# A retention head's epsilon moved to VectorE, and the gates' scalings of two heads moved behind later evictions

## The chip, the cores and the metric

The kernel runs on one core of one Trainium2 chip. Its engines work side by side, each through its own queue in order: TensorE (matrix products, PE in the profile, with its weight loads as PEld), VectorE (DVE), ScalarE (ACT), GpSimd (POOL) and SyncE (SP, which here only asks for transfers). The metric is the time of one execution on the device in microseconds. Lower is better.

## What is computed

Two layers of an encoder over 512 frames of width 1024, in float32. Each layer norms its input, multiplies it by one large matrix, and feeds two branches: four mLSTM heads, and four retention heads of value width 512. Both are merged through gates, and a feed-forward part and an embedding follow. The change concerns the retention branch, cut here to its core:

```python
def head_layernorm(y, g, n_heads):          # per frame and head, over 512 values
    mu = jnp.mean(yf, axis=-1, keepdims=True)
    var = jnp.mean(jnp.square(yf - mu), axis=-1, keepdims=True)
    yn = ((yf - mu) * lax.rsqrt(var + EPS)).reshape(B, S, W)
    return yn * g.astype(jnp.float32)
...
hr = retention_chunkwise(rq4, rk4, rv, log_gamma)
y_r = silu(rg) * head_layernorm(hr, r_norm_g[i], R_HEADS)
merged = sigmoid(gm) * (y_m @ w_bm[i]) + sigmoid(gr) * (y_r @ w_br[i])
```

## The kernel before

The 512 frames are held as 4 blocks of 128. Every product with a float32 operand is made as three matmuls of a high and a low part (`fp32r`). So each weight that is loaded (tiles `wr`) is split before use: ScalarE copies the high part (L309), VectorE subtracts it for the low part (L310), into tiles `w`, `w_A` to `w_D` or `w_t` with three slots of the large kind. TensorE needs both parts.

Most large products are formed by seven partial products, P1 to P7 (one level of Strassen's scheme). `run_pair` makes them for two column tiles at a time in the order P1, P5, P6, P2, P3, P7, with P4 put off to the next `flush()`. `run_wide` makes them for values and gates, 2 heads at a time, in two halves `u` each, P1 and P5 first, then P6 and P2 in turns, then P7, P3, P4. After a product `done` takes it out of PSUM: P1, P6 and P7 and P4 share a bank "a", so P6 can't start before P1 has been taken out, and P4 not before P7. In `pair_tiles` these evictions are lines 610 to 622, inside `ahead()`, which raises their priority.

The order in which an engine works is made at compile time from the order of the program text, priorities and dependencies. The text order is one input to it and not the order itself.

Retention heads are handled in turn. `r_attend` multiplies scores by values, one block `j` after the other: TensorE makes the block, ScalarE copies it to `num[:, j, :]` (L845), and `each(j)` follows:
- VectorE takes the statistics of the block (`bn_stats` L1154, `bn_aggr` L1155) into `mv`
- GpSimd adds EPS to the variance (L1157) and raises it to -1/2 (L1158) into `hv`, both 128x1
- where a gate is given, `r_gate` for an earlier block: ScalarE scales the gate by `hv` (L1200), VectorE forms (num - mean) x gate in place (L1201)

Gates come from `r_gates` for two heads at once. For the first and the third head of a layer (`r_attend(0, ...)` and `r_attend(2, ...)`, which end before) `r_gate` follows each finished gate within `r_gates`. The second and the fourth head (`r_attend(1, ...)` and `r_attend(3, ...)`, which come after) get the other gate `g` as an argument, and each runs `r_gate` for blocks 0 and 1 inside `each(2)` and `each(3)`. What remains comes behind: for the second head blocks 2 and 3 right after `r_attend`, ahead of the next value products `rv_vals(2)`; for the fourth head behind P6 and P2 of the first gr pair. `r_out` then transposes `num` on TensorE (L867): for the second head in the middle of `rv_vals(2)` (ahead of P7), for the fourth right after P7 of the gr pair, with P4 of that pair flushed after the first group of transposes.

GpSimd also asks for the transfers that add weight blocks in DRAM (L367, tiles `s...t`), each of which waits for a certain matmul. VectorE forms the last operands of `rv_vals` itself (L474).

The tiles `y` of `rv_vals` and `r_gates` take turns in four buffers of the tags `qkh` and `qkl`, in the order in which they are made. The gates `g` are such tiles.

Of the kernel before, what the change touches and what calls it, by code (L numbers as in the profile page):

```python
# [35 lines left out]
F32 = mybir.dt.float32  # L36
F32R = mybir.dt.float32r
AF = mybir.ActivationFunctionType
OP = mybir.AluOpType
# [3 lines left out]
P = 128  # L43
T = 512
NT = T // P
# [4 lines left out]
EPS = 1e-6  # L50
# [203 lines left out]
def build(ctx, tc, ins, out):  # L254
    nc = tc.nc
    ve, ac, gp, te = nc.vector, nc.scalar, nc.gpsimd, nc.tensor
# [17 lines left out]
    cur = {}  # L274
# [96 lines left out]
    def pace():  # L371
        if at["step"] < len(steps) and at["credit"] >= 0:
            step()
# [6 lines left out]
    def next_unit():  # L380
        n = at["unit"]
        at["unit"] += 1
        tick("FULL" if full(n) and units[n][0] == "PAIR" else units[n][0])
        return n
# [130 lines left out]
    def flush():  # L515

        while later:
            later.pop()()
# [35 lines left out]
            product(x)  # L554
        later.append(last)

    def run_wide(name, act, done, mid=None):

        n = next_unit()
        assert units[n][0] == "WIDE", units[n]  # L560
        bank = {}
        for x, u in TURNS:
            y, j = WIDE[x]
            if u and x != "P6":
                tick("WIDE")
            if (x, u) == ("P6", 0):
                flush()
            if (x, u) == ("P7", 0) and mid:
                mid()
            b = {"P2": "b", "P5": "c", "P3": "c"}.get(x, "a")  # L570
            first = x in ("P1", "P2", "P5")
            if first and u == 0:
                bank[b] = [ps(f"{name}{b}{t}") for t in range(2)]
            ready(place[n, (y, u)] + LOOK)
            wh, wl = pieces.pop((n, (y, u)))
            for k in (2 * u, 2 * u + 1):
                h, l = act[k](j)
                s = slice(k % 2 * T, (k % 2 + 1) * T)
                f, e = first and k == 0, k == 3
                for t in range(2):  # L580
                    ts = slice(t * P, (t + 1) * P)
                    o = bank[b][t]
                    te.matmul(o, h[:, ts], wh[:, s], start=f, stop=False, skip_group_check=True)
                    te.matmul(o, h[:, ts], wl[:, s], start=False, stop=False, skip_group_check=True)
                    cur["mm"] = te.matmul(o, l[:, ts], wh[:, s], start=False, stop=e, skip_group_check=True)  # L585
            if u:
                for t in range(2):
                    done(x, t, bank[b][t])
            pace()

    def ahead():
# [369 lines left out]
    x = big("x0", F32)  # L961
# [22 lines left out]
    for i in range(L):  # L984
# [38 lines left out]
        for k in range(KT):  # L1023
            s = slice(k * P, (k + 1) * P)
            f, e = k == 0, k == KT - 1
# [119 lines left out]
        def r_attend(h, pt, vv, g=None):  # L1145
            nm = f"l{i}r{h}"
            num = cur["low"].tile([P, NT, 512], F32, name=f"{nm}num", tag="num")
            st = cols.tile([P, NT, 6], F32, name=f"{nm}st", tag="st")
            mv = cols.tile([P, NT, 2], F32, name=f"{nm}mv", tag="mv")
            hv = cols.tile([P, NT], F32, name=f"{nm}hv", tag="hv")  # L1150
            norm = num, mv, hv

            def each(j):
                ve.bn_stats(st[:, j, :], num[:, j, :])  # L1154
                ve.bn_aggr(mv[:, j, :], st[:, j, :])  # L1155
                c = hv[:, j:j + 1]
                gp.tensor_scalar(c, mv[:, j, 1:2], EPS, None, OP.add)  # L1157
                gp.tensor_tensor(c, c, nhalf[:, 0:1], OP.pow)  # L1158
                if g and j > 1:
                    r_gate(norm, g, j - 2)  # L1160

            attend(nm, pt, vv[0], vv[1], 0, 512, num, each)
            return norm
# [33 lines left out]
        def r_gate(norm, g, j):  # L1197

            num, mv, hv = norm
            ac.activation(g[j], g[j], AF.Copy, scale=hv[:, j:j + 1])  # L1200
            ve.scalar_tensor_tensor(num[:, j, :], num[:, j, :], mv[:, j, 0:1], g[j], OP.subtract, OP.mult)  # L1201

        def r_out(h, num, y):
            nm = f"l{i}r{h}o"
            for v in range(4):
                o = back(nm, num, v)
                if v == 0:
                    flush()
                k = (4 * h) % 8 + v
                c = bcol(i, "grn", 4 * h + v)  # L1210
                ac.activation(y[0][k], o, AF.Copy, scale=c)
                ve.scalar_tensor_tensor(y[1][k], o, c, y[0][k].bitcast(F32), OP.mult, OP.subtract)
# [15 lines left out]
        low = cur["br"].tile([P, KT, T], F32R, name=f"l{i}xnl", tag="xn")  # L1228
# [21 lines left out]
            return [[cur["low"].tile([P, 576], F32R, name=f"{nm}v{a}{j}", tag=f"v{a}", bufs=NT) for j in range(NT)]  # L1250
                    for a in "hl"]

        def rv_vals(h, mid=None):

            nm = f"l{i}r{h}"
            bv = [tmp(f"{nm}bv{d}") for d in range(2)]
            for d in range(2):
                nc.sync.dma_start(bv[d], bias_rows(1024 + (h + d) * 512))
            y = [[cur["low"].tile([P, T], F32, name=f"{nm}y{d}{j}", tag="qk" + "hl"[d], bufs=4) for j in range(NT)]
                 for d in range(2)]  # L1260
            v = value_tiles(nm)

            def head0(j):
                split(y[0][j], v[0][j][:, :T], v[1][j][:, :T])

            def head1(j):
                gp.dma_start(rv_dram[i, h // 2, j], y[1][j])

            def done(x, t, o):
                a, b = t, 2 + t  # L1270
                if x == "P1":
                    ve.tensor_tensor(y[0][b], o, bv[0], OP.add)
                elif x == "P2":
                    ve.tensor_tensor(y[0][b], o, y[0][b], OP.add)
                    head0(b)
                elif x == "P4":
                    ve.tensor_tensor(y[0][a], o, bv[0], OP.add)
                    head0(a)
                elif x == "P5":
                    ve.tensor_tensor(y[1][a], o, bv[1], OP.subtract)  # L1280
                elif x == "P6":
                    ve.tensor_tensor(y[1][b], o, bv[1], OP.subtract)
                elif x == "P3":
                    ve.scalar_tensor_tensor(y[1][b], o, -1.0, y[1][b], OP.mult, OP.subtract)
                    head1(b)
                else:
                    ve.scalar_tensor_tensor(y[1][a], o, -1.0, y[1][a], OP.mult, OP.subtract)
                    head1(a)

            run_wide(f"{nm}v", xs, done, mid)  # L1290
            return v

        def rv_fetch(h):
# [11 lines left out]
        qk = qk_tiles(f"l{i}m0")  # L1305
# [15 lines left out]
        vv = mv_vals(0, xa, n1.c)  # L1321
# [4 lines left out]
        pt = m_scores(0, qk)  # L1326
        qk = m_qk(1, xa, n1, xn_tile)
        num = m_attend(0, pt, vv)
# [9 lines left out]
        xs = sevenfold(xn, xs_t)  # L1338
        pt = m_scores(1, qk)
        qk = m_qk(2, xn, None)  # L1340
        xs_sums(0)
        num = m_attend(1, pt, vv)
        gs = m_gates(1, xn, None)
        vv = mv_vals(1, xn, None, lambda: m_back(1, gs, num))
        xs_sums(1)
        pt = m_scores(2, qk)
        qk = m_qk(3, xn, None)
        xs_sums(2)
        num = m_attend(2, pt, vv)
# [4 lines left out]
        pt = m_scores(3, qk)  # L1354
        gs = m_gates(3, xn, None)
        num = m_attend(3, pt, vv)
        vv = rv_vals(0, lambda: m_back(3, gs, num))


# [15 lines left out]
        qk = r_qk(0)  # L1375
# [4 lines left out]
        pt = r_scores(0, qk)  # L1380
        qk = r_qk(1)
        num = r_attend(0, pt, vv)
        vv = rv_fetch(1)
        pt = r_scores(1, qk)
        g = r_gates(0, num, lambda: rv_split(vv))
        yr = acts(cur["br"], f"l{i}yr0")
        r_out(0, num[0], yr)
        num = r_attend(1, pt, vv, g)
        for j in (2, 3):
            r_gate(num, g, j)  # L1390
        vv = rv_vals(2, lambda: r_out(1, num[0], yr))
        qk = r_qk(2)

        def br_tiles(c0, c1):
# [7 lines left out]
        pt = r_scores(2, qk)  # L1402
        qk = r_qk(3)
        num = r_attend(2, pt, vv)
        vv = rv_fetch(3)
        br_tiles(4, 8)
        pt = r_scores(3, qk)
        g = r_gates(2, num, lambda: rv_split(vv))
        yr = acts(cur["br"], f"l{i}yr1")
        r_out(2, num[0], yr)  # L1410
        num = r_attend(3, pt, vv, g)
        mh, ml = [], []
        gr = {}

        def gr_gates(p, then=None):
            def consume(g):
                for d in range(2):
                    ac.activation(g[d], g[d], AF.Sigmoid, bias=bcol(i, "bgr", 2 * p + d), scale=SIGN[d])
                    gr[2 * p + d] = g[d]

            pair_tiles(f"l{i}gr{p}", xs, consume, then=then)

        gr_gates(0, {"P6": lambda: r_gate(num, g, 2), "P2": lambda: r_gate(num, g, 3)})
        r_out(3, num[0], yr)
        for c in range(KT):
            if c and c % 2 == 0:
# [3 lines left out]
            u = tmp(f"l{i}bml{c}")  # L1430
# [15 lines left out]
        if i == L - 1:  # L1446
            x_pool = phase("x", act_side)
            whole = x_pool.tile([P, KT, T], F32, name=f"l{i}x", tag="x")
            x = [whole[:, c, :] for c in range(KT)]
        else:  # L1450
            x = big(f"l{i}x", F32)
# [355 lines left out]
```

## Time and profile before

| | us |
|---|---|
| median of 3 runs | 2301.65 |
| lowest, highest | 2300.31, 2305.29 |
| the profiled execution | 2302.19 |
| its span in the profile | 2300.5 |

The profile is of one execution. It gives busy times by engine, a list of waits (who waited for whom, total, times, longest), and the instructions of each engine in order of time: start, duration, engine, line, operation, output and inputs, and in brackets the idle time before it with what ended it. Matmuls are pipelined: the duration of one overlaps the next, and the pace is read from their starts. The durations on GpSimd are rough. Tiles are named by layer and head, counted from 0: `l0r1num` is `num` of layer 0, second retention head; `l0gr0` the first gr pair; `l0r2v` the value products of `rv_vals(2)`.

### The profile page before, as it was taken

What the parts mean: (1) busy time and instruction counts of PE and PEld (TensorE: products, weight loads), DVE (VectorE), ACT (ScalarE), POOL (GpSimd) and SP (SyncE); (2) the same over time, 40 slices, a digit from 0 to 9 for tenths busy, and PEclk for the clock granted to TensorE, in tenths of its full rate; (3) what the DMA queues carried; (4) which work ended last, traced back from release to release, by engine and by line L of the source; (5) the groups of instructions that cost most, each with busy time, mean ns of one, the idle gap of its engine ahead of it and who ended that gap; (6) DMA issues with size and microseconds to landing.
All of it is one profiled execution on the core that took longest, in us unless ns stands there. A gap on an engine that the chain in (4) does not pass through costs nothing.

```text
span 2300.5 us, 36407 instructions
## 1 busy us (share of the span) xinstructions
PE 2277.2 (99%) x13532; PEld 2020.8 (88%) x13532; DVE 1759.0 (76%) x2690; ACT 1266.5 (55%) x1835; POOL 616.2 (27%) x984
## 2 busy tenths in 40 slices
PE   9999999999999999999999999999999999999998
PEld 7888899888888899999888888988888888999997
DVE  7877767886676878788779687777867678787785
ACT  6766544554554546556557564445545446566564
POOL 3332222223124322223432332221232242111112
PEclk9999999999999999999999999999999999999999
DMA  6776787787789888888886768876877898878741
GB/s 211 189 195 175 243 234 215 209 235 211 233 228 268 220 229 229 239 239 210 227 227 183 196 177 250 232 213 220 228 221 208 244 266 217 246 233 232 236 161 56
DMA packets 187890, 499.33 MB, mean 217 GB/s; under 512 B 26352, under 2 KB 29808, under 8 KB 187712
## 3 DMA queue, kind: packets, MB, share of 16 engines
q0 software_dynamic: 57520, 188.53, 36.9%
q1 hardware_dynamic: 114496, 280.97, 36.2%
q10 hardware_dynamic: 15696, 27.50, 3.6%
q8 instruction: 106, 1.74, 0.3%
q14 instruction: 72, 0.59, 0.1%
HBM read 478.03 MB, written 194.51 MB: 292 GB/s over the span
## 4 chain that ended last, share of the span: by engine, by line
PE 85%; DVE 7%; ACT 2%; issue 2%; DMA 2%; POOL 1%; SPq 0%; DVEq 0%; ACTq 0%; POOLq 0%
PE l0f L488 1%; PE l0f L489 1%; PE l0f L490 1%; PE l0br L488 1%; PE l1br L488 1%; PE l1br L490 1%; PE l0br L490 1%; PE l1br L489 1%; PE l0br L489 1%; DVE w_B L310 1%; PE l1f L488 1%; PE l1f L490 1%; PE l1f L489 1%; DVE w_C L310 1%; PE l0pg L488 1%
## 5 line engine op out<-in xcount | busy, mean ns | idle before, releaser
L309 ACT ACTIVATE w<-wr 128x1024 fp32r<-128x1024 f32 (+1 forms) x193 | 199.7, 1042 | 125.9 <-issue 28.5
L310 DVE TENSOR_TENSOR w<-wr,w 128x1024 fp32r<-128x1024 f32 (+1 forms) x193 | 233.8, 1214 | 45.3 <-ACT w L309 44.7
L309 ACT ACTIVATE w_B<-wr 128x1024 fp32r<-128x1024 f32 x123 | 130.4, 1060 | 150.5 <-PE l0bm L490 13.1
L310 DVE TENSOR_TENSOR w_B<-wr,w_B 128x1024 fp32r<-128x1024 f32 x123 | 150.0, 1221 | 55.0 <-ACT w_B L309 54.5
L309 ACT ACTIVATE w_C<-wr 128x1024 fp32r<-128x1024 f32 x75 | 79.3, 1057 | 66.8 <-issue 9.6
L310 DVE TENSOR_TENSOR w_C<-wr,w_C 128x1024 fp32r<-128x1024 f32 x75 | 92.4, 1233 | 25.0 <-ACT w_C L309 21.0
L309 ACT ACTIVATE w_A<-wr 128x1024 fp32r<-128x1024 f32 x75 | 79.0, 1054 | 46.6 <-DMA wr<-wpairs 4.4
L310 DVE TENSOR_TENSOR w_A<-wr,w_A 128x1024 fp32r<-128x1024 f32 x75 | 91.6, 1222 | 14.2 <-ACT w_A L309 12.0
L309 ACT ACTIVATE w_t<-wr 128x1024 fp32r<-128x1024 f32 x56 | 59.1, 1059 | 61.8 <-PE l0g2va L585 6.3
L309 ACT ACTIVATE w_D<-wr 128x512 fp32r<-128x512 f32 x75 | 47.3, 631 | 81.6 <-DVE wr L470 26.7
L310 DVE TENSOR_TENSOR w_t<-wr,w_t 128x1024 fp32r<-128x1024 f32 x56 | 68.4, 1221 | 19.7 <-ACT w_t L309 19.1
L488 PE MATMUL l0f<-l0n2h,w 128*128 128x512 f32 x176 | 68.7, 390 | 0.0
L490 PE MATMUL l0f<-l0n2h,w 128*128 128x512 f32 x176 | 68.5, 389 | 0.0
L489 PE MATMUL l0f<-l0n2l,w 128*128 128x512 f32 x176 | 68.5, 389 | 0.0
L310 DVE TENSOR_TENSOR w_D<-wr,w_D 128x512 fp32r<-128x512 f32 x75 | 51.7, 689 | 15.1 <-ACT w_D L309 14.6
L367 POOL DMA_DIRECT2D s30t<-wpairs x24 | 16.8, 700 | 91.9 <-PE l1o20a L541 9.0
L490 PEld LDWEIGHTS l0f<-l0n2h,w 128*128 128x128 f32 x176 | 33.0, 188 | 7.0
L488 PEld LDWEIGHTS l0f<-l0n2h,w 128*128 128x128 f32 x176 | 33.0, 188 | 6.5
L489 PEld LDWEIGHTS l0f<-l0n2l,w 128*128 128x128 f32 x176 | 33.0, 188 | 6.4
L488 PE MATMUL l1f<-l1n2h,w 128*128 128x512 f32 x96 | 37.6, 391 | 0.0
L490 PE MATMUL l1f<-l1n2h,w 128*128 128x512 f32 x96 | 37.4, 390 | 0.0
L489 PE MATMUL l1f<-l1n2l,w 128*128 128x512 f32 x96 | 37.4, 389 | 0.0
(5796 smaller groups left out, 9085.3 us busy)
## 6 DMA issues: line engine op xcount, KB each, us to landing
wr<-wstream SPq DMA_DIRECT2D x189, 512.0 KB, 4.9
wr<-wpairs SPq DMA_DIRECT2D x225, 256.0 KB, 4.1
wr<-wwide SPq DMA_DIRECT2D x48, 512.0 KB, 4.6
s3t<-wwide POOLq DMA_DIRECT2D x24, 256.0 KB, 4.3
s6t<-wwide POOLq DMA_DIRECT2D x24, 256.0 KB, 5.2
s18t<-wwide POOLq DMA_DIRECT2D x24, 256.0 KB, 5.1
s21t<-wwide POOLq DMA_DIRECT2D x24, 256.0 KB, 5.1
s24t<-wpairs POOLq DMA_DIRECT2D x24, 256.0 KB, 5.7
```

The lines of the kernel that those rows point to most:

```text
L309: a = ac.activation(hi_ap, src, AF.Copy)
L310: return a, ve.tensor_sub(lo_ap, src, hi_ap.bitcast(F32))
L367: dma = gp.dma_start(piece(g, x, p, q), piece(g, MADE[x][a], p, q), max_dma_last_dim=4096, **kw)
L488: te.matmul(o, sh, mh, start=first, stop=False)
L489: te.matmul(o, sh, ml, start=False, stop=False)
L490: cur["mm"] = te.matmul(o, sl, mh, start=False, stop=last)
```

## The change

EPS is added by VectorE instead of GpSimd, in all four heads of both layers. `run_wide` gets an argument `then`, a call behind a given half of a product. The scalings of blocks 2 and 3 of the second head are asked for behind the second half of P1 (after its evictions) and the first half of P5 of `rv_vals(2)`. For the fourth head all four scalings leave `r_attend` or the places behind P6 and P2, and are asked for behind P5, P6, P2 and P3 of the first gr pair. In `rv_vals` the y tiles are made in the order 2, 3, 0, 1, so that the tiles of P1 (blocks 2 and 3) get the buffers of gates 0 and 1.

```diff
-    def run_wide(name, act, done, mid=None):
+    def run_wide(name, act, done, mid=None, then=None):
...
             if u:
                 for t in range(2):
                     done(x, t, bank[b][t])
+            if then and (x, u) in then:
+                then[x, u]()
             pace()
...
                 c = hv[:, j:j + 1]
-                gp.tensor_scalar(c, mv[:, j, 1:2], EPS, None, OP.add)
+                ve.tensor_scalar(c, mv[:, j, 1:2], EPS, None, OP.add)
                 gp.tensor_tensor(c, c, nhalf[:, 0:1], OP.pow)
...
-        def rv_vals(h, mid=None):
+        def rv_vals(h, mid=None, then=None):
...
-            y = [[cur["low"].tile([P, T], F32, name=f"{nm}y{d}{j}", tag="qk" + "hl"[d], bufs=4) for j in range(NT)]
+            y = [{j: cur["low"].tile([P, T], F32, name=f"{nm}y{d}{j}", tag="qk" + "hl"[d], bufs=4) for j in (2, 3, 0, 1)}
...
-            run_wide(f"{nm}v", xs, done, mid)
+            run_wide(f"{nm}v", xs, done, mid, then)
...
         num = r_attend(1, pt, vv, g)
-        for j in (2, 3):
-            r_gate(num, g, j)
-        vv = rv_vals(2, lambda: r_out(1, num[0], yr))
+        vv = rv_vals(2, lambda: r_out(1, num[0], yr),
+                     {("P1", 1): lambda: r_gate(num, g, 2), ("P5", 0): lambda: r_gate(num, g, 3)})
...
-        num = r_attend(3, pt, vv, g)
+        num = r_attend(3, pt, vv)
...
-        gr_gates(0, {"P6": lambda: r_gate(num, g, 2), "P2": lambda: r_gate(num, g, 3)})
+        gr_gates(0, {x: lambda j=j: r_gate(num, g, j) for j, x in enumerate(("P5", "P6", "P2", "P3"))})
```

## The prediction, made before the result

> **What bounds the kernel now.** I read the page first, for the bound, then the waits of TensorE alone, then the order in time of each engine around those waits.
>
> ```profile
> span 2300.5 us, 36407 instructions
> PE 2277.2 (99%) x13532; PEld 2020.8 (88%) x13532; DVE 1759.0 (76%) x2690; ACT 1266.5 (55%) x1835; POOL 616.2 (27%) x984
> ```
>
> TensorE is busy for 2277.2 of 2300.5 us, so a change elsewhere can only win what TensorE loses by waiting. The waits of TensorE, longest first, name eight at the places that the change touches (us in total, times, longest):
>
> ```profile
> PE l0gr0a L539 <- ACT l0gr0y L610: 1.1, 1, 1.1
> ...
> PE l1gr0a L539 <- ACT l1gr0y L610: 0.8, 1, 0.8
> PE l1r2vc L584 <- DVE w_t L310: 0.8, 1, 0.8
> ...
> PE l0r2vc L584 <- DVE w_t L310: 0.8, 1, 0.8
> PE l0gr0a L539 <- DVE l0gr0y L620: 0.7, 1, 0.7
> PE l1gr0a L539 <- DVE l1gr0y L620: 0.7, 1, 0.7
> PE l0r2vc L583 <- ACT w_t L309: 0.7, 1, 0.7
> PE l1r2vc L583 <- ACT w_t L309: 0.7, 1, 0.7
> ```
>
> They come in three places, once a layer: the value products behind the second head (r2v), the product P6 of the first gr pair behind the fourth head (released by L610), and P4 of that pair (released by L620). A wait as listed is shorter than what TensorE loses, for the modelled end of the matmul before it covers part. The starts tell the loss. Second head, layer 0 (start, us, instruction):
>
> ```profile
> 455.63 0.39 PE L585 MATMUL l0r2vc<-w_t,l0xsl 128*128 128x512 f32 x1
> 456.75 0.51 PE L583 MATMUL l0r2vc<-w_t,l0xsh 128*128 128x512 f32 x1 [0.74 <-ACT w_t L309]
> 458.01 0.50 PE L584 MATMUL l0r2vc<-w_t,l0xsh 128*128 128x512 f32 x1 [0.75 <-DVE w_t L310]
> 458.35 0.40 PE L585 MATMUL l0r2vc<-w_t,l0xsl 128*128 128x512 f32 x1
> 458.58 0.39 PE L583 MATMUL l0r2vc<-w_t,l0xsh 128*128 128x512 f32 x1
> ```
>
> The last pair starts 0.23 apart, the pace without a wait. From 455.63 to 458.35 are three such steps, 0.68, and took 2.72: 2.04 lost. Why the weights w_t came late is seen in the order of ScalarE, GpSimd and VectorE (in brackets: idle time before, and what ended it):
>
> ```profile
> 450.12 0.72 ACT L1200 ACTIVATE l0g0y<-l0g0y,l0r1hv 128x512 f32<-128x512 f32 x1 [1.42 <-POOL l0r1hv L1158]
> 450.75 0.58 ACT L845 ACTIVATE l0r1num<-l0r1a 128x512 f32<-128x512 f32 x1
> 455.03 0.72 ACT L1200 ACTIVATE l0g0y<-l0g0y,l0r1hv 128x512 f32<-128x512 f32 x1 [3.70 <-POOL l0r1hv L1158]
> 455.66 1.99 ACT L309 ACTIVATE w_t<-wr 128x1024 fp32r<-128x1024 f32 x2
> ...
> 448.69 1.40 POOL L1158 TENSOR_TENSOR l0r1hv<-l0r1hv,nhalf 128x1 f32<-128x1 f32 x1
> ...
> 452.90 0.62 POOL L1157 TENSOR_SCALAR l0r1hv<-l0r1mv 128x1 f32<-128x1 f32 x1 [1.97 <-DVE l0r1mv L1155]
> 453.60 1.40 POOL L1158 TENSOR_TENSOR l0r1hv<-l0r1hv,nhalf 128x1 f32<-128x1 f32 x1
> ...
> 453.35 1.22 DVE L474 TENSOR_TENSOR t<-wr,wr 128x1024 f32<-128x1024 f32 x1
> ```
>
> The third scaling (450.12) stands ahead of the fourth block's eviction L845, which makes the fourth block's statistics late; the fourth scaling then holds ScalarE idle for 3.70 us, with the split of w_t behind it. Fourth head, layer 0:
>
> ```profile
> 636.23 0.28 PE L541 MATMUL l0gr0c<-l0xsh,w_A 128*128 128x256 f32 x1
> 637.61 0.39 PE L539 MATMUL l0gr0a<-l0xsh,w_B 128*128 128x256 f32 x1 [1.10 <-ACT l0gr0y L610]
> ...
> 637.97 0.28 PE L541 MATMUL l0gr0a<-l0xsh,w_B 128*128 128x256 f32 x1
> 638.08 0.28 PE L539 MATMUL l0gr0a<-l0xsh,w_B 128*128 128x256 f32 x1
> ...
> 643.44 0.71 PE L867 MATMUL l0r3ot<-ident,l0r3num 128*128 128x128 f32 x5
> 644.89 0.39 PE L539 MATMUL l0gr0a<-l0xnh,w_D 128*128 128x256 f32 x1 [0.74 <-DVE l0gr0y L620]
> ...
> 636.56 0.72 ACT L1200 ACTIVATE l0g2y<-l0g2y,l0r3hv 128x512 f32<-128x512 f32 x1 [1.07 <-POOL l0r3hv L1158]
> 637.19 0.36 ACT L610 ACTIVATE l0gr0y<-l0gr0a 128x256 f32<-128x256 f32 x1
> ...
> 635.19 0.69 POOL L1157 TENSOR_SCALAR l0r3hv<-l0r3mv 128x1 f32<-128x1 f32 x1
> 635.96 0.57 POOL L1158 TENSOR_TENSOR l0r3hv<-l0r3hv,nhalf 128x1 f32<-128x1 f32 x1
> ```
>
> P6 adds into the bank of P1, which L610 must empty first, and L610 stands behind the third scaling, which waits for GpSimd. Without a wait a step is 0.115 (637.97 to 638.08); 636.23 to 637.97 took 1.74 for three steps, 0.35: 1.39 lost. P4 loses about 1.0: the five transposes take 0.71 with the last one's 0.27, so P4 could have started near 643.95 and did at 644.89, with a slow first step.
>
> **The change part by part.**
>
> The scalings of blocks 2 and 3 of the second head are asked for behind P1's eviction and behind half of P5, so w_t's split, the eviction L845 and P1's eviction have the earlier place. If ScalarE follows, the 3.70 us of idle time ahead of the split go, more than the 2.04 that are lost, as long as the split's slot is free by then. I take the whole loss: 2.04 in layer 0, and the waits of layer 1 are the same 0.7 and 0.8, so 4.1 for both. Bounds: 0 to 4.1 won. What becomes late next are the scalings, and nothing needs their blocks before the transposes L867:
>
> ```profile
> L867 PE MATMUL l0r1ot<-ident,l0r1num x16: 270/272/273, 471.5 to 473.2; 128*128 128x128 f32 x16
> ```
>
> That is 15 us after the end of the last scaling today, 455.03 + 0.72. The new order of the y tiles gives the evictions of P1 the buffers of gates 0 and 1, whose scalings come early; without it they would wait for the moved ones. Beyond that it is worth nothing: the buffers serve the next q and k only after a whole pair of products. 0, both ends.
>
> In the fourth head all four scalings move behind P5, P6, P2 and P3, out of the way of L845 and L610. Then P1 is emptied while P5 runs, and P6's wait goes: 1.39, and 1.1 in layer 1, whose wait is 0.3 shorter: 2.5. Bounds: 0 to 2.5 won. P4's wait hangs on VectorE's work between P5 and P4. Two products L1201 of about 0.75 come into that stretch, where VectorE stood idle 1.52 before one of them (its idle time ended by the scaling):
>
> ```profile
> 640.26 0.75 DVE L1201 SCALAR_TENSOR_TENSOR l0r3num<-l0r3num,l0r3mv,l0g2y 128x512 f32<-128x512 f32 x1 [1.52 <-ACT l0g2y L1200]
> ```
>
> They fit the idle time, so I take 0; the ends are 2.0 won (the wait gone in both layers) and 3.0 lost (4 x 0.75 with no idle time to take them).
>
> The epsilon: 32 additions of 128x1 leave GpSimd for VectorE. The nearest row there:
>
> ```profile
> L730 DVE TENSOR_SCALAR l1n41ms<-l1n41ss x2: 157/158/159, 2291.2 to 2291.4; 128x1 f32<-128x1 f32 x2
> ```
>
> 32 x 0.158 is 5.1 us of VectorE. In the chain to a scaling the step shortens: 0.70 between the starts 452.90 and 453.60 becomes about 0.16. In the first head, where the chain's end is needed only much later, TensorE does not wait at all (PE busy 15.00 of 15.00 us; then PEld, DVE):
>
> ```profile
> 395.00:410.00 15.00, 15.00 (x75) 12.82 (x74) 13.27 (x27) 8.50 (x15) 7.25 (x16) 1.00 0.64 200
> ```
>
> VectorE has 1.7 us spare there for four additions of 0.6 together, and the third head is built alike. I take 0 on the path; the ends are 0 and 5.1 lost, if that cover is gone. The Trainium skill (VectorE: DVE Perf Modes, Rules for kernel authors) speaks against this edit: it says to keep the number of VectorE instructions small, as each pays a flush of the pipe. By it the sum would be the 5.1 dearer end; the window above speaks for the cheap one.
>
> Sum: 4.1 + 2.5 = 6.6 won. The profiled execution took 2302.19 us (span 2300.5), 0.5 above the median 2301.65; from it the sum gives 2295.6, and against the median 2295.1.
>
> **The rivals.**
>
> A, the scalings keep their places on ScalarE. For it: the third scaling of the fourth head is already written behind P6's eviction, yet ran at 636.56 ahead of L610, the eviction of P1. The written place does not bind the engine's order. Then only the additions help. In the second head the fourth block's step of 0.70 becomes 0.16, 0.54 won, and about as much at the third block ahead of it, 1.1 a layer. In the fourth head the third power could start at 635.19 instead of 635.96, 0.8 a layer. Both layers: 3.8, which gives 2297.9. The powers stay slow, 1.40 instead of 0.57 where L474 runs beside them. The Trainium skill (SBUF — State Buffer, Who interferes with whom) says that a VectorE instruction with two SBUF inputs and a GpSimd one that reads SBUF shut each other out; the trace agrees with 1.40 beside L474. Against A: with the scalings later in the text they lose every tie.
>
> B, the win is given back at the fourth head. The last scaling is asked for behind P3, and one product later, 12 x 0.115 = 1.4 us, the transposes need it. With two splits of w ahead of it (1.05 each on ScalarE, as half of the 1.99 above) and the product on VectorE it is done 2 x 1.05 + 0.72 + 0.75 = 3.6 after P3, so TensorE waits about 2.2 a layer, 4.4: 2299.5.
>
> C, slower. The same place, one mechanism: ScalarE's next work goes ahead of all four scalings.
>
> ```profile
> 643.64 1.06 ACT L309 ACTIVATE w_A<-wr 128x1024 fp32r<-128x1024 f32 x1 [0.98 <-PE l0gr0a L541]
> 644.72 1.28 ACT L1418 ACT_TABLE_LOAD   x1
> 646.01 0.72 ACT L1418 ACTIVATE l0gr0y<-l0gr0y,bc 128x512 f32<-128x512 f32 x1
> ```
>
> This starts 0.2 after P7's end and takes 3.1, four scalings of 0.72 take 2.9 and a product 0.75: the transposes would wait 6.9 a layer, P4's 1.0 is covered by it, so 11.8 - 6.6 = 5.2 lost: 2306.9. It decides from a wait of about 6.6 us a layer on. Against it: in the trace scalings run early, not late.
>
> D, the additions are paid in full on VectorE: 2295.1 + 5.1 = 2300.2.
>
> **How the numbers follow.** The forecast has a chance of 0.58, and its own range is 2292 to 2297.5 (P4's wait gone, and the runs' lowest 1.3 under their median, on the one side, half of the second head's win lost on the other). A has 0.20, B 0.11, D 0.03, C 0.08. A measurement of this kernel can tell about 0.2%, 4.6 us, from no change: 2297.0 to 2306.3 is the same. Nearly all of the forecast's cases lie under 2297.0, 0.54, and a few of A's, 0.03: faster 0.57. C and little else is slower: 0.09. The rest is the same, 0.34. The range takes in A, B and D up to 2301 and leaves C out.
>
> **What would show it.** Right: the waits of TensorE for w_t in r2vc and for L610 are gone in both layers; the idle times of ScalarE before L1200, 3.70 at the fourth block, are gone or have only other scalings behind them; L1201's last product in the fourth head ends before P7 does. Wrong: L1200 still ahead of L845 and L610 (A), a wait of L867 for num (B, C), or waits of TensorE for splits at other heads (D). The prediction also fails if the new order moves waits to places that I have not priced.

## The result, and the profile after

| | us |
|---|---|
| before, median of 6 runs | 2301.98 (2300.31 to 2305.97) |
| after, median of 6 runs | 2292.65 (2290.9 to 2294.26) |
| ratio after to before | 0.9957, 95% interval 0.9946 to 0.9967 |
| after, the profiled execution and its span | 2292.93, 2291.2 |

The change wins 9.3 us by the medians, 0.41%, and 0.43% by the ratio of the runs. In the kernel after, the lines of the file stand two lower from the middle of the file on: EPS is L1159, the power L1160, the scaling L1202, the product L1203, the copy of a block L847, the evictions of P1 and P5 L612 and L614.

The page after, first lines:

```profile
span 2291.2 us, 36395 instructions
PE 2273.9 (99%) x13532; PEld 2019.5 (88%) x13532; DVE 1761.7 (77%) x2722; ACT 1266.5 (55%) x1835; POOL 607.7 (27%) x952
```

32 instructions went from POOL to DVE (984 to 952, 2690 to 2722). The two longest waits of TensorE after:

```profile
PE l1n41ss L728 <- POOL l1n41sum L705: 1.2, 1, 1.2
PE warm L971 <- POOL ones_r L298: 1.1, 1, 1.1
```

None of the eight waits at the second and fourth heads is left. ScalarE in the second head of layer 0, after:

```profile
445.82 1.34 ACT L1202 ACTIVATE l0g0y<-l0g0y,l0r1hv 128x512 f32<-128x512 f32 x2 [1.62 <-POOL l0r1hv L1160]
447.07 0.57 ACT L847 ACTIVATE l0r1num<-l0r1a 128x512 f32<-128x512 f32 x1
447.55 0.71 ACT L1202 ACTIVATE l0g0y<-l0g0y,l0r1hv 128x512 f32<-128x512 f32 x1
449.04 1.07 ACT L309 ACTIVATE w_t<-wr 128x1024 fp32r<-128x1024 f32 x1 [0.78 <-PE l0r2va L585]
453.24 0.73 ACT L1202 ACTIVATE l0g0y<-l0g0y,l0r1hv 128x512 f32<-128x512 f32 x1 [3.13 <-POOL l0r1hv L1160]
453.87 1.04 ACT L309 ACTIVATE w_t<-wr 128x1024 fp32r<-128x1024 f32 x1
```

The copy L847 of block 3 now stands ahead of the third scaling, and the first split of w_t (449.04) ahead of the fourth. The fourth scaling still holds ScalarE for 3.13 us, but the split behind it is one that TensorE needs later. The fourth head, TensorE after:

```profile
632.60 0.28 PE L541 MATMUL l0gr0c<-l0xsh,w_A 128*128 128x256 f32 x1
632.98 0.39 PE L539 MATMUL l0gr0a<-l0xsh,w_B 128*128 128x256 f32 x1
...
633.32 0.28 PE L541 MATMUL l0gr0a<-l0xsh,w_B 128*128 128x256 f32 x1
...
638.65 0.71 PE L869 MATMUL l0r3ot<-ident,l0r3num 128*128 128x128 f32 x5
639.33 0.39 PE L539 MATMUL l0gr0a<-l0xnh,w_D 128*128 128x256 f32 x1
```

P6 starts 0.38 behind P1's last matmul instead of 1.38, and P4 0.68 behind the start of the transposes instead of 1.45.

To see where time is won I compare, at each place, how long TensorE takes from the first to the last start of the products there (tiles `r2va` and `gr0a`) with the same stretch before. For layer 0's second head the ends are these rows of the tile's instructions, the earliest and the latest group, first before, then after (in a row: the duration of one in ns, minimum, median, maximum, then the first and the last start):

```profile
L583 PE MATMUL l0r2va<-w_B,l0xnh x8: 389/389/389, 447.7 to 452.5; 128*128 128x512 f32 x8
...
L585 PE MATMUL l0r2va<-w_t,l0xnl x8: 389/389/391, 484.6 to 489.4; 128*128 128x512 f32 x8
```

```profile
L583 PE MATMUL l0r2va<-w_B,l0xnh x8: 389/389/389, 446.1 to 450.9; 128*128 128x512 f32 x8
...
L585 PE MATMUL l0r2va<-w_t,l0xnl x8: 389/389/391, 481.0 to 485.7; 128*128 128x512 f32 x8
```

447.7 to 489.4 is 41.7, 446.1 to 485.7 is 39.6: 2.1 won. All kernels of this document, worked out in the same way from starts to 0.01 us or finer (us against before, minus is won):

| kernel | second head, layer 0, 1 | fourth head, layer 0, 1 | sum | median of all runs |
|---|---|---|---|---|
| after | -2.1, -2.0 | -1.9, -2.0 | -8.0 | 2292.65 |
| `moves_only` | +1.7, 0.0 | 0.0, 0.0 | +1.7 | 2302.32 |
| `eps_only` | -1.6, -1.6 | -1.5, -2.0 | -6.7 | 2294.76 |
| `order_after_gpsimd` | -2.1, -2.0 | -2.3, -2.0 | -8.4 | 2293.73 |
| `order_before_vector` | -1.1, -1.1 | +0.5, 0.0 | -1.7 | 2298.97 |
| `four_adds_gpsimd` | +1.7, +3.3 | +5.2, +4.3 | +14.5 | 2315.25 |
| `two_adds_vector` | -2.1, -2.0 | -1.8, -0.7 | -6.6 | 2294.03 |
| `eps_and_second_head` | -2.1, -2.0 | -1.5, -2.0 | -7.6 | 2292.74 |
| `eps_and_fourth_head` | -1.6, -1.6 | -1.9, -2.0 | -7.2 | 2294.37 |

The places come from one execution each. A further 0.8 to 1.6 us lies at the very start in all of them against before, `moves_only` too: the profiled execution of before waited there for a normed input, long before the first place of the change (1.04 us ahead of the matmul at 9.08).

### The profile page after: what moved, and what is told of

Its sections match the earlier page's. It is cut to its first block, busy times and chain, and to the rows that moved or that the text cites. A ratio compares the mean times of both kernels' runs of the same rounds, so it can differ in the third digit from the quotient of the medians.

```text
span 2291.2 us, 36395 instructions
## 1 busy us (share of the span) xinstructions
PE 2273.9 (99%) x13532; PEld 2019.5 (88%) x13532; DVE 1761.7 (77%) x2722; ACT 1266.5 (55%) x1835; POOL 607.7 (27%) x952
## 3 DMA queue, kind: packets, MB, share of 16 engines
q8 instruction: 106, 1.74, 0.3%
## 4 chain that ended last, share of the span: by engine, by line
PE 88%; DVE 6%; ACT 2%; issue 2%; DMA 2%; POOL 0%; DVEq 0%; SPq 0%; ACTq 0%; POOLq 0%
PE l0f L488 1%; PE l0f L489 1%; PE l0f L490 1%; PE l1br L488 1%; PE l0br L488 1%; PE l0br L490 1%; PE l1br L490 1%; PE l1br L489 1%; PE l0br L489 1%; PE l1f L488 1%; PE l1f L490 1%; PE l1f L489 1%; DVE w_B L310 1%; PE l0pg L488 1%; PE l0pg L490 1%
## 5 line engine op out<-in xcount | busy, mean ns | idle before, releaser
L310 DVE TENSOR_TENSOR w<-wr,w 128x1024 fp32r<-128x1024 f32 (+1 forms) x193 | 234.1, 1216 | 44.5 <-ACT w L309 43.7
L310 DVE TENSOR_TENSOR w_B<-wr,w_B 128x1024 fp32r<-128x1024 f32 x123 | 150.2, 1222 | 53.5 <-ACT w_B L309 53.0
L310 DVE TENSOR_TENSOR w_C<-wr,w_C 128x1024 fp32r<-128x1024 f32 x75 | 92.5, 1233 | 26.2 <-ACT w_C L309 22.5
L310 DVE TENSOR_TENSOR w_A<-wr,w_A 128x1024 fp32r<-128x1024 f32 x75 | 91.7, 1223 | 13.7 <-ACT w_A L309 11.1
L310 DVE TENSOR_TENSOR w_t<-wr,w_t 128x1024 fp32r<-128x1024 f32 x56 | 68.2, 1222 | 21.0 <-ACT w_t L309 20.4
L310 DVE TENSOR_TENSOR w_D<-wr,w_D 128x512 fp32r<-128x512 f32 x75 | 51.7, 690 | 15.3 <-ACT w_D L309 14.8
```

Of the source, the lines that this page charges most:

```text
L310: return a, ve.tensor_sub(lo_ap, src, hi_ap.bitcast(F32))
```

## The experiments

Four theories are weighed in them: M, that the moved text wins the time, as predicted; E, that the epsilon's edit does; O, that ScalarE's compiled order does, whatever made it; and G, that it is the time of the additions on GpSimd.

**The moves alone.** The kernel after with EPS back on GpSimd:

```diff
-                ve.tensor_scalar(c, mv[:, j, 1:2], EPS, None, OP.add)
+                gp.tensor_scalar(c, mv[:, j, 1:2], EPS, None, OP.add)
```

> The scalings of the second and fourth head moved in the text and the y tiles reordered as in the changed kernel, the epsilon left on GpSimd. Theory M (the later places in the text let ScalarE run the split of w_t and the evictions first): 6.6 to 8 us faster than before, TensorE's waits for w_t in r2v and for L610 gone. Theory E (the engines' order follows from where the epsilon is added, not from the text's places): no change, within 1.5 us of before, all eight waits of TensorE back with 0.7 to 1.1 us each, and the third scaling of the second head again ahead of the eviction L845 of the fourth block.

Measured 2302.32 (11 runs) against 2301.52 before, ratio 1.0001 (0.9992 to 1.001). The waits of TensorE there, in this kernel:

```profile
PE l0gr0a L539 <- ACT l0gr0y L612: 1.1, 1, 1.1
...
PE l1gr0a L539 <- ACT l1gr0y L612: 0.8, 1, 0.8
PE l1r2vc L584 <- DVE w_t L310: 0.8, 1, 0.8
PE l0r2vc L584 <- DVE w_t L310: 0.8, 1, 0.8
```

The eight waits at the two heads are back with the sizes of before. The compiled program has every instruction of every engine in the place that it has before; the moves of both heads and the new order of the y tiles changed no engine's order.

**The epsilon alone.** The kernel before with this one line:

```diff
-                gp.tensor_scalar(c, mv[:, j, 1:2], EPS, None, OP.add)
+                ve.tensor_scalar(c, mv[:, j, 1:2], EPS, None, OP.add)
```

> Only the epsilon goes to VectorE; no scaling moves in the text. Theory M: at most the 3.8 us of rival A (the steps of 0.70 us become 0.16), so 2298 or later, with part of the wait for w_t left. Theory E: 7 to 9 us faster, second head 2.1 us a layer won as in the changed kernel, fourth head 1 to 2 us a layer; the third scaling of the second head behind the eviction of the fourth block and the fourth scaling behind the split of w_t.

Measured 2294.76 (5 runs), ratio 0.9968 (0.9955 to 0.998): 6.8 of the 9.3 us, just short of theory E's 7 to 9. ScalarE's compiled order is that of the kernel after; VectorE's differs from it in the place of one product L1201 in each of the two heads, and GpSimd's in the place of one request for a transfer in the fourth head. One wait is left at the two heads, 0.6 for P1's eviction in the fourth head of layer 0. So it is the epsilon's edit that made the order which the moves ask for.

**Order and additions taken apart.** Two kernels fix ScalarE's order with explicit ordering edges within that engine's queue (`behind(b, a)` puts `b` behind `a`). The first has the moves, EPS on GpSimd and the order of after:

```diff
+        def second(j):
+            s = r_gate(num, g, j)
+            behind(s, copied if j == 2 else cur["split"])
...
+            if j:
+                behind(s, (copied4, cur["P1"], cur["split"])[j - 1])
```

> The epsilon stays on GpSimd, and ScalarE is held by order edges to the order that the changed kernel has: third scaling of the second head behind the eviction of the fourth block, fourth behind the split of w_t; in the fourth head second scaling behind the eviction, third behind P1's eviction, fourth behind the split of w. Theory O (what counts is the order of ScalarE's queue, so that no weight split and no eviction waits behind a scaling): 7 to 9 us faster, as the changed kernel. Theory C (what counts is that the chain to the scaling is shorter without GpSimd's additions): 0 to 3 us faster, since GpSimd still adds, and TensorE still waits in both places.

Measured 2293.73 (5 runs), ratio 0.9961 (0.9949 to 0.9974); no wait of TensorE is left at the two heads. GpSimd works in the order of before there; on VectorE the products L1201 behind the moved scalings went later as well. The second kernel has EPS on VectorE and the scalings ahead of the copy, of w_t's split and of P1's evictions, as before, though one split of w in the fourth head comes earlier than there:

```diff
+                if j == 2:
+                    for k in range(soon):
+                        cur["scaled"] = r_gate(norm, g, k)
...
+                behind(copied, cur.pop("scaled"))
...
+                behind(both_[0], cur.pop("first"))
```

> The epsilon is added by VectorE, and ScalarE is held by order edges to the order of the kernel before (third scaling of the second head ahead of the fourth block's eviction, fourth ahead of the split of w_t; in the fourth head the third scaling ahead of P1's eviction and the fourth ahead of P5's). Theory O: most of the win is gone; what is left is rival A's, up to 3.8 us, and TensorE waits for w_t in r2v. Theory C: 7 to 9 us faster, as the changed kernel.

Measured 2298.97 (11 runs), ratio 0.999 (0.9982 to 0.9999). Its waits of TensorE (lines of its own file; L616 evicts P1, L618 P5):

```profile
PE l0gr0a L545 <- ACT l0gr0y L616: 1.4, 1, 1.4
...
PE l0gr0c L545 <- ACT l0gr0y L618: 0.8, 1, 0.8
PE l1gr0c L545 <- ACT l1gr0y L618: 0.8, 1, 0.8
PE l1r2vc L590 <- DVE w_t L310: 0.6, 1, 0.6
PE l0r2vc L590 <- DVE w_t L310: 0.6, 1, 0.6
```

So with the addition left on GpSimd the order alone wins what the whole change wins, and the cheaper addition without the order wins 1.1 a layer in the second head. The fourth head of this kernel does not price the addition: its order is not quite that of before. TensorE makes two matmuls of P2 ahead of P6, P4 no longer waits, and P3 waits 0.8 for P5's eviction, which stands behind the fourth scaling.

**How far the order carries.** The kernel before, with EPS added in four quarters on GpSimd:

```diff
-                gp.tensor_scalar(c, mv[:, j, 1:2], EPS, None, OP.add)
+                gp.tensor_scalar(c, mv[:, j, 1:2], EPS / 4, None, OP.add)
+                gp.tensor_scalar(c, c, EPS / 4, None, OP.add)
+                gp.tensor_scalar(c, c, EPS / 4, None, OP.add)
+                gp.tensor_scalar(c, c, EPS / 4, None, OP.add)
```

> The kernel before, with one edit: the epsilon is added in four quarters, all four on GpSimd, so that GpSimd gets 96 instructions more and VectorE none. The compiled program puts the scalings of the second head in the places on ScalarE that they have in the kernel after (the third behind the copy of block 3, the fourth behind the split of w_t), and one scaling of the fourth head three places later than before. Theory O (ScalarE's compiled order decides, not which engine adds): the second head wins about 2.0 us a layer as in the kernel after, the fourth 0 to 1.9, so 2302.0 - 4.0 to - 7.8 = 2294.2 to 2298.0, in spite of more work on GpSimd; the wait of l1r2vc and l0r2va for w_t is gone. Theory G (what helps is the time that the additions cost on GpSimd, 0.22 to 1.24 us each, rival A's account): three more additions per block make the scalings later, and the time rises by 0.8 to 4.0 us a layer at the places of the waits, 2303 to 2310.

Measured 2315.25 (5 runs) against 2301.79, ratio 1.0057 (1.0044 to 1.007). The expectation by theory O was wrong by 17 us or more, and theory G's range ended at 2310. ScalarE in the second head of this kernel:

```profile
446.75 0.72 ACT L1203 ACTIVATE l0g0y<-l0g0y,l0r1hv 128x512 f32<-128x512 f32 x1 [2.12 <-POOL l0r1hv L1161]
450.71 0.72 ACT L1203 ACTIVATE l0g0y<-l0g0y,l0r1hv 128x512 f32<-128x512 f32 x1 [3.24 <-POOL l0r1hv L1161]
451.34 0.58 ACT L845 ACTIVATE l0r1num<-l0r1a 128x512 f32<-128x512 f32 x1
451.82 0.71 ACT L1203 ACTIVATE l0g0y<-l0g0y,l0r1hv 128x512 f32<-128x512 f32 x1
452.44 1.05 ACT L309 ACTIVATE w_t<-wr 128x1024 fp32r<-128x1024 f32 x1
457.34 0.72 ACT L1203 ACTIVATE l0g0y<-l0g0y,l0r1hv 128x512 f32<-128x512 f32 x1 [3.86 <-POOL l0r1hv L1161]
```

The third and fourth scalings stand in the places that they have after. But now the second one makes ScalarE wait 3.24, and the copy of block 3 stands behind that one: 451.34, where it was at 447.07 after. GpSimd shows why:

```profile
446.80 0.22 POOL L1157 TENSOR_SCALAR l0r1hv<-l0r1mv 128x1 f32<-128x1 f32 x1
...
447.39 0.21 POOL L1157 TENSOR_SCALAR l0r1hv<-l0r1mv 128x1 f32<-128x1 f32 x1
447.68 0.64 POOL L1159 TENSOR_SCALAR l0r1hv<-l0r1hv 128x1 f32<-128x1 f32 x1
448.40 1.05 POOL L1158 TENSOR_SCALAR l0r1hv<-l0r1hv 128x1 f32<-128x1 f32 x1
```

L1157 comes twice, for the second and the third block, before the second block's L1159: the additions of two blocks take turns, and one took 1.05. An order helps only as far as what stands in front is ready. So neither theory holds alone: the order decides which work a late scaling holds up, and the additions on GpSimd decide how late it is. In the fourth head, TensorE waits 4.78 for P1's eviction behind the third scaling, and more follows from the wait itself (see the last section).

**Additions on VectorE priced.** The kernel after with EPS in two halves, both on VectorE:

```diff
-                ve.tensor_scalar(c, mv[:, j, 1:2], EPS, None, OP.add)
+                ve.tensor_scalar(c, mv[:, j, 1:2], EPS / 2, None, OP.add)
+                ve.tensor_scalar(c, c, EPS / 2, None, OP.add)
```

> The kernel after, with one edit: the epsilon is added in two halves, both on VectorE, 32 more additions. ScalarE's compiled order is that of the kernel after. The prediction's step (additions on VectorE lie beside other work, 0 on the path): 2292.65 within 1 us. Rival D's account (additions are paid in full on VectorE): 32 x 0.148 = 4.7 us more, 2297.4.

Measured 2294.03 (6 runs, 2292.71 to 2295.25), ratio 0.9964 (0.9952 to 0.9976), 1.4 above after, which the intervals do not separate; it is 0.4 more than the prediction's step allowed. All of its six runs lie below the 2297.4 of full price. In the trace the loss is at one place, the fourth head of layer 1, where P4 waits 0.7 again. The power of the fourth block took 1.47 there (0.99 after), and the fourth scaling held ScalarE idle for 1.75 (0.56 after).

**The two moves, each with the epsilon.** The kernel after with the fourth head's text as before, and the kernel after with the second head's (there the y tiles have their old order too):

```diff
-        num = r_attend(3, pt, vv)
+        num = r_attend(3, pt, vv, g)
...
-        gr_gates(0, {x: lambda j=j: r_gate(num, g, j) for j, x in enumerate(("P5", "P6", "P2", "P3"))})
+        gr_gates(0, {"P6": lambda: r_gate(num, g, 2), "P2": lambda: r_gate(num, g, 3)})
```

> The kernel after without its fourth-head part: epsilon on VectorE, the second head's two scalings asked for behind P1 and half of P5 and the y tiles in their new order; the fourth head asks for its scalings as before. ScalarE's compiled order is that of the kernel after; only one product on VectorE in the fourth head has another place. Theory O: the second head -2.1 a layer as after, the fourth head between that of the epsilon alone (-1.5, -1.9) and after (-1.9, -2.0): 2292.7 to 2294. Theory M (the text's moves are worth something of their own): the fourth head would lose its part of the move, 2.5 a layer by the prediction, 2297.7.

```diff
-        vv = rv_vals(2, lambda: r_out(1, num[0], yr),
-                     {("P1", 1): lambda: r_gate(num, g, 2), ("P5", 0): lambda: r_gate(num, g, 3)})
+        for j in (2, 3):
+            r_gate(num, g, j)
+        vv = rv_vals(2, lambda: r_out(1, num[0], yr))
```

> The kernel after without its second-head part: epsilon on VectorE, the fourth head's scalings asked for behind P5, P6, P2 and P3; the second head asks for its third and fourth scaling as before and the y tiles keep their order. ScalarE's compiled order is that of the kernel after; one product on VectorE in the second head of layer 0 has another place. Theory O: second head -1.6 to -2.1 a layer, fourth -1.9 to -2.0: 2292.7 to 2294. Theory M: the second head would lose 2.04 a layer by the prediction, 2296.7.

Measured 2292.74 (ratio 0.9962, 0.9949 to 0.9974) and 2294.37 (0.9966, 0.9954 to 0.9979), 5 runs each. Neither loses a whole move's worth, as theory M would have it; the second is 0.4 above theory O's range. In the traces the second head still wins 0.4 a layer more where its text is moved (-2.1 and -2.0 against -1.6). They also show by what. VectorE in the second head of layer 1, in `eps_and_fourth_head`, and then in the kernel after:

```profile
1587.34 1.21 DVE L474 TENSOR_TENSOR t<-wr,wr 128x1024 f32<-128x1024 f32 x1
1589.77 0.75 DVE L1201 SCALAR_TENSOR_TENSOR l1r1num<-l1r1num,l1r1mv,l1g0y 128x512 f32<-128x512 f32 x1 [1.22 <-ACT l1g0y L1200]
1590.43 1.22 DVE L310 TENSOR_TENSOR w_t<-wr,w_t 128x1024 fp32r<-128x1024 f32 x1
```

```profile
1587.09 1.22 DVE L474 TENSOR_TENSOR t<-wr,wr 128x1024 f32<-128x1024 f32 x1
1588.23 1.22 DVE L310 TENSOR_TENSOR w_t<-wr,w_t 128x1024 fp32r<-128x1024 f32 x1
...
1592.76 0.75 DVE L1203 SCALAR_TENSOR_TENSOR l1r1num<-l1r1num,l1r1mv,l1g0y 128x512 f32<-128x512 f32 x1
```

With the text moved, the last product stands behind the low part of w_t (L310) and no longer in front of it, so the low part comes 2.0 earlier, counted from the head's first product (1583.03 and 1582.79). That is 0.9 for both layers; the fourth head's move adds at most 0.5, in layer 0. By the times alone these shares can't be told from nothing.

## Why the prediction was right in its number and wrong in its cause

The predicted 2295.1 stands against 2292.65, inside the range and inside the forecast's own range, on the faster side. That the number was right is in part luck: the edit that was priced at nothing brought the order that the moves were credited with, and a term that was too large stood against one that was too small. By its steps:

- **The step that failed** is "If ScalarE follows, the 3.70 us of idle time ahead of the split go", which I granted to the text, and so did "with the scalings later in the text they lose every tie". ScalarE did not follow: the moves alone compile to the program of before. It followed when the epsilon changed engines. Even then the idle time did not go, though the sign under "What would show it" asked for that: 3.13 us are left ahead of the fourth scaling, and only what stands behind them has changed. Rival A named the right rule, "The written place does not bind the engine's order", and had the wrong consequence, "Then only the additions help" with 3.8 us: moving the additions moved the order as well. With the order held, the additions alone won 2.2 in the second head, as A's 1.1 a layer says; A's 0.8 a layer in the fourth is not tested, for TensorE's order differs there. The medians differ by 2.5 (2301.52 to 2298.97).
- **The second head, 4.1**: 4.1 in the trace. The size came from what TensorE lost and held whatever the cause: about 3.2 by the epsilon's edit, 0.9 by the text.
- **P6, 2.5**: in layer 0 the three steps from P1's last matmul took 0.72 (632.60 to 633.32) instead of 1.74. Without a wait they take 0.35, so 0.37 of the 1.39 is still lost and 1.02 was won. In layer 1 the whole 1.1 was won, 2.1 for both.
- **P4, taken as 0**, is the mis-sized term. From the start of the fifth transpose to that of P4 TensorE took 1.01 before (643.88 to 644.89) and 0.24 after (639.09 to 639.33), so 0.8 of the 1.9 that the fourth head won in layer 0 came from P4; the last 0.1 is P3, which had started with a slow step. Layer 1 won as much at P4. The prediction saw idle time of VectorE that the products could fill, and not why VectorE was late. Before, the fourth scaling kept ScalarE idle with a split of w behind it, and VectorE's half of that split and the eviction L620 came late in turn:

```profile
639.50 0.72 ACT L1200 ACTIVATE l0g2y<-l0g2y,l0r3hv 128x512 f32<-128x512 f32 x1 [1.95 <-POOL l0r3hv L1158]
...
640.39 1.05 ACT L309 ACTIVATE w<-wr 128x1024 fp32r<-128x1024 f32 x1
...
641.48 1.23 DVE L310 TENSOR_TENSOR w<-wr,w 128x1024 fp32r<-128x1024 f32 x1 [0.47 <-ACT w L309]
...
644.42 0.41 DVE L620 TENSOR_TENSOR l0gr0y<-l0gr0a,l0gr0y 128x256 f32<-128x256 f32 x1
```

  After, that split (633.70) stands ahead of the fourth scaling (634.95). The last product on VectorE ended before P7 did, as "What would show it" asked, and left VectorE free for what P4 waits for. VectorE after, with the eviction L622 right behind P7's last matmul (638.53 + 0.28):

```profile
635.93 0.74 DVE L1203 SCALAR_TENSOR_TENSOR l0r3num<-l0r3num,l0r3mv,l0g2y 128x512 f32<-128x512 f32 x1
...
638.85 0.42 DVE L622 TENSOR_TENSOR l0gr0y<-l0gr0a,l0gr0y 128x256 f32<-128x256 f32 x1
```

  P4 won 1.5 for both layers, of the 2.0 at the good end of that term. The places add up to 4.1 + 2.1 + 1.5 and 0.3 at P3, 8.0 in all; of the 2.4 by which the time came out under the forecast, 1.4 is this difference between 6.6 and 8.0, and the rest is less than the runs scatter.
- **The epsilon on VectorE, 0 on the path**: held for the price of the additions, though not for the edit as a whole, which brought the order. The row after is a little cheaper than the one that I took (0.158): one addition is 0.134 to 0.154.

```profile
L1159 DVE TENSOR_SCALAR l0r1hv<-l0r1mv x4: 136/148/154, 444.9 to 450.4; 128x1 f32<-128x1 f32 x4
```

  The rule of the Trainium skill (VectorE: DVE Perf Modes, Rules for kernel authors) to keep the count of VectorE operations small would have charged these additions; 32 more of them cost 1.4 of 4.7 us here by the medians, so the runs do not bear it out at the full price of an addition.
- **"0, both ends" for the y tiles' order**: the moved text alone, with this order in it, gave the same program, so it cost and won nothing there. Beside the rest of the change, the old order of the tiles compiles to the same order of every engine; it was not timed.
- **Rivals B and C** did not come: no wait for `num` at L869. (B's 1.05 for a split is not half of the 1.99 that it points at, which is 1.0, but the row of w_A under C has 1.06.) **D** is out too: the time is 7.5 under its 2300.2.

Why the compiler's order turns on one small instruction stays argued, not shown. The runs show that changing what stands in the chain to `hv` changes where scalings and products are put (one addition off GpSimd moves scalings back, and so do three additions more there), as a scheduler would that puts instructions down by when it thinks them ready.

## What to carry to other kernels

Before a place in the text is priced, see whether the compiled order of the engine moves with it; if the order is made by a scheduler, an edit that shortens a chain can move other instructions, and this side effect may be the larger part (here about 4 of 6.8 us, if the 2.5 that the additions won with the order held are the direct part). An in-order engine that waits for a late scalar loses nothing by itself (the 3.13 us that are left here cost TensorE nothing): look at what stands directly behind the waiting instruction, put the work that TensorE needs next in front, and keep the chain short, since the order is good only while what stands in front is ready. Where a forecast rests on one cause for a loss, run the parts of the edit one by one, for the sum can be right with the cause wrong.

## What the runs showed of the hardware that I had not expected

A long wait of TensorE costs more than the wait. After the 4.78 us in `four_adds_gpsimd`, TensorE at the first two matmuls of P6 and at the first one back at full pace, and then the busy times of a stretch behind the wait (its length, PE, PEld, DVE, ACT, POOL, the granted clock, then the share and rate of transfers):

```profile
641.82 0.58 PE L539 MATMUL l0gr0a<-l0xsh,w_B 128*128 128x256 f32 x1 [4.78 <-ACT l0gr0y L610]
642.20 0.41 PE L540 MATMUL l0gr0a<-l0xsl,w_B 128*128 128x256 f32 x1
...
647.11 0.30 PE L539 MATMUL l0gr0c<-l0xsh,w_C 128*128 128x256 f32 x1
```

```profile
641.70:643.10 1.40, 1.28 (x6) 1.28 (x7) 0.66 (x2) 1.29 (x3) 1.22 (x3) 0.50 0.71 181
```

The clock was 0.50, and a step 0.213 instead of 0.115, up to 647.11: 24 steps of 0.1 more, about 2.4 us. In layer 1 it lasted for some 16 steps, 1.6. Without these the fourth head loses 2.8 and 2.7, the same in both layers. The Trainium skill (TensorE: Matmul & The Clock Gate, Part 1: The HAM clock gate) says that the array falls to half its clock after an idle window of about 3.4 us and needs as long a busy stretch to come back; the 4.78 us and 0.50 agree. The way back took 5.3 us in layer 0 (641.82 to 647.11) and 3.5 in layer 1. But a dip came without such a gap too, in the second head of layer 0 in `moves_only`, where the single waits are below 1 us:

```profile
458.00:461.00 3.00, 3.00 (x9) 2.26 (x9) 3.00 (x4) 0.00 (x0) 0.00 (x0) 0.53 0.65 179
```

Before, around the same place:

```profile
458.00:464.00 6.00, 5.99 (x26) 4.99 (x27) 5.75 (x7) 2.10 (x3) 0.86 (x1) 1.00 0.65 213
```

3.00 us at 0.53 lose 1.4, and the next 3.00 at 0.91 lose 0.3 more, together the +1.7 of `moves_only` there, with the same instructions and waits as before, where the clock stayed at 1.00. In `four_adds_gpsimd` the second head of layer 1 lost 1.6 more than that of layer 0: the clock was 0.59 from 1609 to 1613, and 1.00 at the same place of layer 0. So a place with several short waits close together can lose such a stretch once and not the next time; that the short waits bring it on is not shown.

The power of 128x1 on GpSimd took 0.57 alone, and after the change 2.60 for one block of the second head in each layer. In layer 0:

```profile
450.43 1.21 DVE L474 TENSOR_TENSOR t<-wr,wr 128x1024 f32<-128x1024 f32 x1
...
450.60 2.60 POOL L1160 TENSOR_TENSOR l0r1hv<-l0r1hv,nhalf 128x1 f32<-128x1 f32 x1 [0.74 <-DVE l0r1hv L1159]
...
451.56 1.21 DVE L310 TENSOR_TENSOR w_t<-wr,w_t 128x1024 fp32r<-128x1024 f32 x1
```

Two operations of VectorE with two inputs ran back to back in that time, 450.43 to 452.77, where the 1.40 of before had one beside it (L474 at 453.35). That the power is let in only behind both would fit these times, and no run took it apart. It cost nothing, since the split in front of the waiting scaling was already done.
